# The gate branch's b tiles and the convolution's projection as pairs, in a new order with attention in larger portions

## The chip, the core and the metric

The kernel runs on one core of a Trainium2 chip. Its metric is the device time of one execution in microseconds. Engines are named as in the profile: PE (TensorE matmuls), PEld (its weight loads), DVE (VectorE), ACT (ScalarE), POOL (GpSimd), SP (SyncE, which only issues transfers here). L109 and the like are lines of the kernel before. L109 is the line of the helper through which nearly all of the ordered instructions go, so groups of that line are told apart by the names of their tiles.

## What is computed

One decoder layer on 512 prompt tokens and 8 x 8 sample tokens (576 columns in all), float32, with D_MODEL = 1024 and D_FF = 2816. Attention is a sliding window of 128 with 16 heads and 4 key/value heads.

```
mod = silu(c) @ w_ada + b_ada                      # sh1, sc1, g1, sh2, sc2, g2
h = rmsnorm(x, norm1_g) * (1 + sc1) + sh1
b, c, xa, q, k, v, ga, gb = split(h @ w_in)        # columns 0, 1024, 2048, 3072, 4096, 4352, 4608, 5632
u  = c * xa
ya = (b * causal_conv3(u)) @ w_conv_out            # convolution branch
o  = sliding_window_attention(q, k, v, sinks)      # with ALiBi
yb = o @ w_attn_out
x  = x + g1 * ((sigmoid(ga) * ya + sigmoid(gb) * yb) @ w_mix_out)
h2 = rmsnorm(x, norm2_g) * (1 + sc2) + sh2
a, val = split(h2 @ w_up)
x  = x + g2 * ((gelu(causal_conv3(a)) * val) @ w_down)
y  = rmsnorm(x, final_g)
```

The last inputs of the two convolutions and the last 128 key and value rows are outputs too.

## The kernel before

**Layout.** Activations lie transposed: a tile has 128 features on the partitions and the 576 tokens (NT) along a row, so `h` is a list of 8 tiles (NK), each as a high and a low part. `split` makes them: ACT copies the source, rounded, into the high part, and DVE subtracts that from the source for the low part. A product is taken in three passes (high x high, high x low, low x high).

**Unpaired products.** `product(w, xs)` makes one tile of 128 output features: 8 steps over k, each of 3 passes on 2 groups of tokens (256 and 320), so 48 matmuls into two PSUM banks. `weights` loads a 1024 x 128 block of weights (512 KB, `raw`, by SP) and splits it into `whi` and `wlo`.

**Pairs.** `pair_product` makes two output tiles at once by a Strassen-like scheme of 7 half products instead of 8. The halves are over the output tiles, over k (0 to 3 and 4 to 7) and over the tokens (HT = 288 each). Each of the 7 parts is 4 k-steps of 3 passes on 288 columns, 84 matmuls in all, which accumulate into the banks X, Z and Y; between parts ACT negates a bank into the next (`minus`), or hands a finished quarter to the caller (`out_a0`, `out_b1`, `out_a1`, `out_b0`). The scheme needs sums of weights: `pair_weights` makes from the two raw blocks the split tiles A (first part, `a0` and `a1`), B (`s1`, `b1`), C (`s2`, `s4`), all 128 x 1024, and D (`s3`, 128 x 512). The second part uses B, the third C. It needs sums of the activations too: `PairOperands`, for each k pair (k, k + 4), adds and subtracts halves on DVE and splits the results (`th`/`tl`, `nh`/`nl`, and `n3`, which overwrites half of h's own tile).

A pair's weight parts are made during the pair before: `steps` maps a part's number to what is issued there on ACT and DVE (`in_turn`: sums and A at 0, B at 2, D at 3, C at 4 or 5). From the gates to tile 3 of attention's projection PE, ACT and DVE run in the order in which the program is written (`pinned`); elsewhere a scheduler may move DVE's and ACT's unpinned instructions.

**Fillers.** `tick()` is called after every k-step. It adds a rate to a sum, and when the sum reaches 1 it takes the next portion of a generator: this is how attention's and the modulation's small matmuls get between the products' matmuls in PE's order. `drain()` issues what is left.

**The stages that the change touches**, in order of time:
1. for each m of 8: the c tile, the x tile (u = c * xa and its convolution: `conv`, two taps on DVE), and the b tile (`conv_times`, split into `g`), each an unpaired product. Beside them, at a rate of 0.58 per tick, `attention`: 16 prompt units (4 key heads x 4 blocks), each as `prompt_scores` (three portions, the last with the softmax) and `prompt_values` (three portions), where the values of a unit come behind the scores of the next; then two decode units. The four aux PSUM banks are shared by them.
2. the convolution's projection: 8 unpaired products of `w_conv_out` with g. Beside them `modulation(2048)` as a filler: rows of w_ada (`ada`, 256 KB each, by SP; two sets ahead), four small matmul groups of 16 at L1100. `PairOperands` of h are made from m = 3 on.
3. eight gate pairs (columns 4608 for the convolution branch, 5632 for attention's), whose sigmoids stay in SBUF; the convolution's tiles are multiplied by theirs (`gated`). In the last pair attention's output is split (`part_o`, tiles `oh` and `ol`).
4. attention's projection: 8 unpaired products of `w_attn_out`, gated and added to ya; beside them `modulation(4096)`, begun at a rate of 2 in 28 during the last pair, then at 11 in 60.
5. x, which the output projection's residual needs, is read back from DRAM into the two tiles that `ot` and `o` had (L1330, 2 x 1152 KB on POOL's queue). Then the output projection and the FFN, whose up-projection is of pairs too, with a convolution and a GELU beside them.

Of the kernel before, what the change touches and what calls it, by code (L numbers as in the profile page):

```python
# [16 lines left out]
P = 128  # L17
# [52 lines left out]
def step_kernel(ctx: ExitStack, tc: tile.TileContext, ins: dict, outs: list):  # L70
# [19 lines left out]
    def slot(s, dt=F32, shape=None):  # L90
        return ap_.tile(shape or [P, NT], dt, tag="a", name=nm(s))
# [31 lines left out]
    def pv(t):  # L123
        return t[:, 0:512]
# [49 lines left out]
    def fill(gen, rate):  # L174
        filler[:] = [gen, rate, 0.0]

    ticks = [0]

    def tick():

        ticks[0] += 1
        if filler:
            filler[2] += filler[1]
            while filler and filler[2] >= 1.0:
                filler[2] -= 1.0
                if next(filler[0], True):
                    filler.clear()
# [94 lines left out]

    def pair_weights(ra, rb):

# [49 lines left out]
    def pair_product(w, x, steps, out_a0, out_a1, out_b0, out_b1):  # L334
# [19 lines left out]

# [616 lines left out]

    def prompt_scores(hd, i, ss, _):
        while 4 * hd + 3 not in QS or ticks[0] < ready[hd]:
            yield False
        w = 256 if i else P
        k0 = (i - 1) * P if i else 0
        ss += [slot("s", shape=[P, 2, 256]) for _ in range(2)]
        kh, kl = (x[:, k0 : k0 + 256] for x in KS[hd])
        for x in range(2):
# [6 lines left out]
            for e in range(2):  # L986
# [4 lines left out]
                )  # L991
            yield False
        softmax(ss, 4, snk[:, 4 * hd : 4 * hd + 4], nsnk[:, 4 * hd : 4 * hd + 4], w)
        yield False

    def prompt_values(hd, i, ss, _):
        nkt = 2 if i else 1
        pts = []
        for kt in range(nkt):
# [10 lines left out]
        yield False  # L1010
        yield False
        O = aux()
        for n in range(2 * nkt):
# [7 lines left out]
            if n:  # L1021
                tc.keep_in_program_order(done)
        yield False
# [4 lines left out]
        yield False  # L1028

    def attention():  # L1030
        units = [(prompt_scores, prompt_values, (hd, i)) for hd in range(4) for i in range(4)]
        units += [(decode_scores, decode_values, (q,)) for q in range(2)]
        before = None
        for n, (sc, va, arg) in enumerate(units + [(None, None, None)]):
            s, more = [], []
            if n in CACHE_AT:
                cache_load(CACHE_AT.index(n))
            if sc is not None:
                yield from sc(*arg, s, more)
            if before is not None:  # L1040
                yield from before
            before = va(*arg, s, more) if va is not None else None


# [101 lines left out]

    def modulations():
        yield from modulation(4096)
# [9 lines left out]
    gcv = []  # L1158
    for m in range(NK):
# [22 lines left out]
        nc.scalar.copy(c_sb, ps)  # L1182
        ps = product(weights(kpm(w_in, 2048 + m * P), NK), h)
        u = padded()
        nc.vector.tensor_tensor(out=u[:, 2:514], in0=pv(ps), in1=pv(c_sb), op=ALU.mult)
        nc.vector.tensor_tensor(
            out=b10(u)[:, :, 2:10], in0=b8(sv(ps)), in1=b8(sv(c_sb)), op=ALU.mult
        )
        keep_state(u, m)
        y = conv(u, parT[:, 64 + m : 65 + m], parT[:, 72 + m : 73 + m], parT[:, 80 + m : 81 + m], stT[:, m, :])  # L1190
        ps = product(weights(kpm(w_in, m * P), NK), h)
        gcv.append(split_slot(conv_times(ps, y), "g"))
    state_out(NK, ncv_p[:], ncv_s[:])


    def sigmoid_pair(w, steps):

        sa, sb = slot("sg"), slot("sg")

        def sigmoid(out, src):  # L1200
            act.activation(out, src, AF.Sigmoid)

        def a0(ps):
            sigmoid(sa[:, :HT], ps)

        def b1(x, y, op):
            dve.tensor_tensor(out=sb[:, HT:], in0=x, in1=y, op=op)

        def a1(x, y, op):
            sigmoid(sb[:, HT:], sb[:, HT:])  # L1210
            dve.tensor_tensor(out=sa[:, HT:], in0=x, in1=y, op=op)

        def b0(ps):
            sigmoid(sb[:, :HT], ps)
            sigmoid(sa[:, HT:], sa[:, HT:])

        pair_product(w, made["op"], steps, a0, a1, b0, b1)
        return [sa, sb]

    ya, made = [], {}  # L1220
    wco, wao = ins["w_conv_out"][0], ins["w_attn_out"][0]
    gate_cols = [c + m * P for c in (4608, 5632) for m in range(0, NK, 2)]
    raws = {}

    def gate_raws(n):
        if n < len(gate_cols):
            raws[n] = [load_w(kpm(w_in, gate_cols[n] + c), NK) for c in (0, P)]

    def conv_out(m, w):
        ps = product(w, gcv)  # L1230
        t = slot("ya")
        act.copy(t, ps)
        ya.append(t)

    for m in range(NK - 1):
        w = weights(kpm(wco, m * P), NK)
        if m >= 3:
            PairOperands(h, m - 3, made).all()
        conv_out(m, w)
    w_last = weights(kpm(wco, (NK - 1) * P), NK)  # L1240
    gate_raws(0)
    pinned += [pe, act, dve]
    w, steps = pair_weights(*raws[0])
    steps = in_turn(steps)
    for n in sorted(steps):
        steps[n]()
    gate_raws(1)
    conv_out(NK - 1, w_last)
    drain()
    sg, o = [], []  # L1250
    w_next = {}

# [3 lines left out]

    def gated(m):

        if sg[m] is not None:
            dve.tensor_tensor(out=ya[m], in0=ya[m], in1=sg[m], op=ALU.mult)  # L1260
            sg[m] = None

    for n in range(len(gate_cols)):
        if n + 1 < len(gate_cols):
            gate_raws(n + 2)
            after, steps = pair_weights(*raws[n + 1])
            steps = in_turn(steps, 5)
            if n >= 4:
                steps[1] = lambda m=2 * n - 8: gated(m)
                steps[4] = lambda m=2 * n - 7: gated(m)  # L1270
        else:
            w_next[0] = weights(kpm(wao, 0), NK)
            raw = load_w(kpm(wao, P), NK)
            steps = {
                0: lambda: gated(6), 1: lambda: gated(7), 3: lambda: part_o(2), 4: lambda: part_o(3),
                5: lambda: w_next.update({1: split_w(raw)}), 6: lambda: part_o(5), 7: lambda: part_o(7),
            }
        if n + 1 == len(gate_cols):
            fill(modulations(), 2 / 28)
        sg += sigmoid_pair(w, steps)  # L1280
        w = after
    part_o(NK)
    gb = sg[NK:]
    filler[1] = 11 / 60
    mixed = []
    for m in range(NK):
        if m + 1 < NK and m + 1 not in w_next:
            w_next[m + 1] = weights(kpm(wao, (m + 1) * P), NK)
        ps = product(w_next.pop(m), o)
        if m == 3:  # L1290
            pinned.clear()
        t = gb[m]
# [35 lines left out]
    x1t = [wp.tile([P, 4, NT], F32, tag="oh", name=nm("x1"), bufs=2) for _ in range(2)]  # L1328
    for x in range(2):
        nc.gpsimd.dma_start(x1t[x], xT_dram[x])  # L1330
    x1 = [x1t[k // 4][:, k % 4, :] for k in range(NK)]
# [516 lines left out]
```

## Time and profile before

| | |
|---|---|
| time, median of 3 runs (lowest, highest) | 1002.71 us (1002.39, 1004.38) |
| the profiled execution's own time | 1002.83 us |
| its span, from first to last instruction | 1001.1 us |
| mean granted clock of TensorE | 0.997 |
| DMA traffic | 119.18 MB, 119 GB/s on the mean |

The stages lie in that execution as follows (from the stretches of the trace; busy us of each engine):

| stage | from, to | PE | DVE | ACT |
|---|---|---|---|---|
| c, x and b tiles with attention | 72 to 324 | 251.79 | 153.61 | 121.80 |
| the convolution's projection | 324 to 383.5 | 59.50 | 30.82 | 18.18 |
| gate pairs | 383.5 to 472.7 | 89.20 | 64.07 | 52.04 |
| start of attention's projection | 473 to 498 | 21.38 | 9.25 | 5.69 |
| rest of it and of the output projection's start | 498 to 540 | 42.00 | 21.75 | 13.00 |

How to read the views: a group's row has line, engine, operation, out<-in with shapes and a count, then busy time and the mean time of one in ns, then the idle time of the engine ahead of these instructions and what ended it. A row of the chain of waits has a start, a length and what the time was spent on, so that consecutive rows are consecutive in time. A row of the DMA issues has the count, the size of each and the median time from issue to landing.

### The profile page before, as it was taken

The page shows a single profiled execution, that of the slowest core. Times are in us where ns is not written, and L with a number is a line of the kernel's source. Part 1 is how long each engine was busy: PE and PEld are TensorE (multiplying, and loading weights), DVE is VectorE, ACT ScalarE, POOL GpSimd, SP SyncE. Part 2 cuts the span into 40 slices and gives each one's busy share as a digit, 9 for nine tenths or more (in the row PEclk, how much of TensorE's full clock was granted, in tenths as well). Part 3 has the DMA queues.
Part 4 walks back from the last instruction along what each step waited for, and adds up shares of the span by engine and source line. Part 5 has one row for each costly group of instructions (what it writes and reads, how often), then busy time and mean ns, then how long its engine had stood idle before and what let it go on. Part 6 is the DMA issues. An engine that isn't in the chain of part 4 may idle for free.

```text
span 1001.1 us, 18626 instructions
## 1 busy us (share of the span) xinstructions
PE 983.0 (98%) x7516; PEld 943.0 (94%) x7516; DVE 642.2 (64%) x1183; ACT 465.2 (46%) x889; POOL 87.7 (9%) x253
## 2 busy tenths in 40 slices
PE   7999999999999999999899999999999999999997
PEld 5799999999999889999689999999999999999997
DVE  5737666666563366786364568995558975579663
ACT  6354545444544225556132338654226663246563
POOL 2222111100010000000000011100000000000020
PEclk9999999999999999999999999999999999999999
DMA  9983322333423822335962402233233322322212
GB/s 294 329 246 98 107 85 77 92 108 112 139 64 95 289 89 84 90 101 160 334 211 71 127 2 64 85 96 95 73 97 102 88 88 82 106 84 85 78 39 95
DMA packets 173480, 119.18 MB, mean 119 GB/s; under 512 B 6887, under 2 KB 160846, under 8 KB 173106
## 3 DMA queue, kind: packets, MB, share of 16 engines
q1 hardware_dynamic: 169954, 107.00, 35.0%
q0 software_dynamic: 3296, 10.73, 3.5%
q8 instruction: 59, 0.97, 0.4%
q14 instruction: 27, 0.22, 0.1%
q10 hardware_dynamic: 144, 0.26, 0.1%
HBM read 109.17 MB, written 7.35 MB: 116 GB/s over the span
## 4 chain that ended last, share of the span: by engine, by line
PE 93%; DMA 3%; issue 1%; SPq 1%; DVE 0%; ACT 0%; POOL 0%; POOLq 0%; DVEq 0%; ACTq 0%
PE mm L109 64%; PE aux L109 27%; PE aux L1100 2%; PE aux L1015 1%; DMA ad<-in_w_ada 1%; DMA ada<-in_w_ada 1%; SPq L381 1%; DMA x<-in_x_prompt 1%; ACT s L866 0%; POOL r L109 0%; DVE cs L388 0%; ACT hh L109 0%; DVE hl L109 0%; DVE yo L109 0%; DVE x L109 0%
## 5 line engine op out<-in xcount | busy, mean ns | idle before, releaser
L109 ACT ACTIVATE whi<-raw 128x1024 fp32r<-128x1024 f32 (+3 forms) x166 | 168.7, 1025 | 197.7 <-PE mm L109 109.8
L109 DVE TENSOR_TENSOR wlo<-raw,whi 128x1024 fp32r<-128x1024 f32 (+3 forms) x166 | 195.2, 1182 | 69.7 <-ACT whi L109 67.6
L109 PE MATMUL mm<-hh,whi 128*128 128x256 f32 (+1 forms) x528 | 118.1, 305 | 0.5 <-ACT hh L109 0.5
L109 PE MATMUL mm<-hh,wlo 128*128 128x256 f32 (+1 forms) x528 | 112.6, 295 | 0.0
L109 PE MATMUL mm<-hl,whi 128*128 128x256 f32 (+1 forms) x528 | 111.6, 295 | 0.1
L109 PEld LDWEIGHTS mm<-hh,whi 128*128 128x128 f32 x528 | 85.6, 188 | 8.1 <-issue 6.6
L109 PEld LDWEIGHTS mm<-hh,wlo 128*128 128x128 f32 x528 | 88.2, 188 | 0.0
L109 PEld LDWEIGHTS mm<-hl,whi 128*128 128x128 f32 x528 | 87.6, 188 | 0.7 <-DVE hl L109 0.5
L109 PE MATMUL aux<-2l,whi 128*128 128x288 f32 (+2 forms) x232 | 68.6, 296 | 0.0
L109 PE MATMUL aux<-2h,wlo 128*128 128x288 f32 (+2 forms) x232 | 68.6, 295 | 0.0
L109 PE MATMUL aux<-2h,whi 128*128 128x288 f32 (+2 forms) x232 | 68.4, 295 | 0.0
L109 PE MATMUL mm<-fh,whi 128*128 128x256 f32 (+1 forms) x304 | 64.8, 295 | 0.3 <-DVE rt L109 0.3
L109 PE MATMUL mm<-fl,whi 128*128 128x256 f32 (+1 forms) x304 | 65.0, 295 | 0.0
L109 PE MATMUL mm<-fh,wlo 128*128 128x256 f32 (+1 forms) x304 | 65.0, 294 | 0.0
L109 DVE SCALAR_TENSOR_TENSOR x<-mm,modT,x 128x512 f32<-128x512 f32 (+1 forms) x33 | 22.6, 685 | 66.0 <-PE mm L109 65.8
L109 PEld LDWEIGHTS mm<-fh,whi 128*128 128x128 f32 x304 | 50.6, 188 | 0.6 <-PE aux L109 0.6
L109 PEld LDWEIGHTS mm<-fh,wlo 128*128 128x128 f32 x304 | 50.9, 188 | 0.0
L109 PEld LDWEIGHTS mm<-fl,whi 128*128 128x128 f32 x304 | 50.8, 188 | 0.0
L866 ACT ACTIVATE s<-s,nmx 128x256 f32<-128x256 f32 (+1 forms) x72 | 34.1, 475 | 25.5 <-DVE nmx L863 17.4
L109 PEld LDWEIGHTS aux<-2h,whi 128*128 128x128 f32 x232 | 43.7, 188 | 0.0
L109 PEld LDWEIGHTS aux<-2l,whi 128*128 128x128 f32 x232 | 43.7, 188 | 0.0
L109 PEld LDWEIGHTS aux<-2h,wlo 128*128 128x128 f32 x232 | 43.6, 188 | 0.0
(314 smaller groups left out, 2581.5 us busy)
## 6 DMA issues: line engine op xcount, KB each, us to landing
raw<-in_w_in SPq DMA_DIRECT2D x52, 512.0 KB, 4.1
raw<-in_w_up SPq DMA_DIRECT2D x44, 512.0 KB, 3.7
ada<-in_w_ada SPq DMA_DIRECT2D x64, 256.0 KB, 6.0
ad<-in_w_ada SPq DMA_DIRECT2D x32, 256.0 KB, 6.1
raw<-in_w_down SPq DMA_DIRECT2D x16, 512.0 KB, 3.4
raw<-in_w_conv_out SPq DMA_DIRECT2D x8, 512.0 KB, 3.5
raw<-in_w_attn_out SPq DMA_DIRECT2D x8, 512.0 KB, 3.6
raw<-in_w_mix_out SPq DMA_DIRECT2D x8, 512.0 KB, 5.7
```

The source lines that it names most:

```text
L109: done = getattr(self.engine, name)(*args, **kwargs)
L381: return tc.keep_in_program_order(nc.sync.dma_start(dst, src))
L866: nc.scalar.activation(s[x // 2][:, x % 2, :w], s[x // 2][:, x % 2, :w], AF.Exp, bias=nmx[:, x : x + 1], accum_out=den[:, x : x + 1],)
L1015: done = nc.tensor.matmul(O[HALF[par], :256], vt(i - nkt + 1 + kt)[:, hd * 64 : hd * 64 + 64], pts[kt][:, par * 256 : par * 256 + 256], st ...
L1100: done = nc.tensor.matmul(ps[32 * j : 32 * j + 32, :], cT[:, k, :], cols[k][j], start=(k == 1), stop=(k == NK - 2),)
```

## The change

- **Order.** The b tiles leave the c/x loop. After c and x come 16 pairs, called jobs: 4 of b tiles (0 to 3), 4 of the gates of attention's branch (4 to 7, columns 5632), 4 of the gates of the convolution's branch (8 to 11, columns 4608), 4 of the convolution's projection (12 to 15). Each job's weights are loaded two jobs ahead and prepared one job ahead.
- **Pairs.** The b tiles and the projection's tiles were unpaired and become pairs. h's `PairOperands` are now made at m = 5 and 6 of the c/x loop, all but `n3`, which job 0 makes (h's own tiles are still needed till then). The projection's operands come from g in plain float32 (`RawOperands`) in small steps laid out by `plan` over jobs 8 to 12.
- **Low parts by DMA.** In `pair_weights`, for the names in `moved`, the low part isn't subtracted on DVE: ACT writes the negated high part into it and POOL's queue adds the source with an accumulating transfer. This is for B and D of the weights of jobs 0 to 4 and 9 to 15.
- **Steps.** D moves to step 3 with the second sums behind it, B to step 1, C's high part to 4 and its low part to 5.
- **Gates.** Sigmoids are stored to DRAM (`sg_dram`, POOL's queue) and read back by SP (`gate`) when they are needed.
- **Fillers.** Attention runs beside c/x alone, a unit in two larger portions (at a rate of 0.3: the scores and softmax; then the values of the unit three before and the transposes of the one two before); decode then at 0.35 and the modulation at 12 in 70. A tick in a pair counts half. `modulation(4096)` starts only after the last job.
- **x's reload** is put under `issue_after` of the tile m = 4 of attention's projection (`x1_after`, a DVE instruction).

```diff
-    def tick():
+    def tick(share=1.0):
         ticks[0] += 1
         if filler:
-            filler[2] += filler[1]
+            filler[2] += filler[1] * share
...
+    class RawOperands:
...
+        def sums(self):
+            (r0, r1), a, b = (self.r0, self.r1), slice(0, HT), slice(HT, NT)
+            self.t = t = slot("tw")
+            dve.tensor_tensor(out=t[:, a], in0=r0[:, a], in1=r0[:, b], op=ALU.subtract)
+            dve.tensor_tensor(out=r0[:, b], in0=r0[:, b], in1=r1[:, b], op=ALU.subtract)
+            dve.tensor_tensor(out=t[:, b], in0=r1[:, b], in1=t[:, a], op=ALU.add)
+        def first(self):
...
+            act.activation(self.x0[0], self.r0, AF.Copy)
...
+        def first_low(self):
...
+            self.low(self.x0, self.r0)
+            dve.tensor_tensor(out=self.r0[:, a], in0=self.r1[:, a], in1=self.t[:, b], op=ALU.subtract)
+        def second(self):
...
+            act.activation(self.tt[0], self.t, AF.Copy)
...
+        def third(self):
...
+            act.activation(self.x1[0], self.r1, AF.Copy)
...
+            act.activation(self.n4[0], self.r0[:, a], AF.Copy)
...
+        def third_low(self):
+            self.low(self.x1, self.r1)
+            self.low(self.n4, self.r0[:, :HT])
...
         def low(name, src):
             hi, lo = w[name]
-            dve.tensor_tensor(out=lo, in0=src, in1=hi.bitcast(F32), op=ALU.subtract)
+            if name in moved:
+                act.activation(lo, hi.bitcast(F32), AF.Copy, scale=-1.0)
+                pool.dma_start(lo.bitcast(F32), src, accum_op=ALU.add)
+            else:
+                dve.tensor_tensor(out=lo, in0=src, in1=hi.bitcast(F32), op=ALU.subtract)
...
-                tick()
+                tick(0.5)
...
     def attention():
...
+        for n in range(len(units) + 3):
...
+            if n < len(units):
+                hd, i = units[n]
+                while 4 * hd + 3 not in QS or ticks[0] < ready[hd]:
+                    yield False
+                s[n] = prompt_scores(hd, i)
+            yield False
+            if n >= 3:
+                prompt_values(*units[n - 3], pts.pop(n - 3))
+            if 2 <= n <= len(units) + 1:
+                pts[n - 2] = prompt_turn(units[n - 2][1], s.pop(n - 2))
+            yield False
+        filler[1] = .35
...
     def beside_conv():
         yield from attention()
-        filler[1] = 13 / 76
+        filler[1] = 12 / 70
         yield from modulation(2048)
         yield True
-    fill(beside_conv(), 0.58)
+    fill(beside_conv(), .3)
+    sg_dram = dp.tile([2, NK, P, NT], F32, name="sg_dram")
...
+        def prepare(self, moved=""):
+            self.w, t = pair_weights(*self.raws, moved=moved)
+            order = {0: "sums1 ah al", 1: "bh bl", 3: "dh dl sums2", 4: "ch", 5: "cl"}
...
+    def branch_outs(m):
+        ts, ys = [slot("g") for _ in range(2)], ycv[m : m + 2]
...
+        def second_half(e, x, y, op):
+            t, v = ts[e], ys[e]
+            dve.tensor_tensor(out=t[:, HT:], in0=x, in1=y, op=op)
+            dve.tensor_tensor(out=t[:, HT:512], in0=t[:, HT:512], in1=v[:, HT:512], op=ALU.mult)
+            nc.gpsimd.tensor_tensor(out=b8(sv(t)), in0=b8(sv(t)), in1=b10(v)[:, :, 0:8], op=ALU.mult)
...
+    def gate_outs(x, m):
...
+        def b0(ps):
+            sigmoid(tb[:, :HT], ps)
+            sigmoid(ta[:, HT:], ta[:, HT:])
+            for e, t in enumerate((ta, tb)):
+                pool.dma_start(sg_dram[x, m + e], t)
...
+    jobs = [Job(w_in, m * P, made, lambda m=m: branch_outs(m)) for m in range(0, NK, 2)]
+    jobs += [
+        Job(w_in, c + m * P, made, lambda x=x, m=m: gate_outs(x, m))
+        for x, c in ((1, 5632), (0, 4608)) for m in range(0, NK, 2)
+    ]
+    jobs += [Job(wco, m * P, made_g, lambda m=m: conv_outs(m)) for m in range(0, NK, 2)]
...
-        ps = product(weights(kpm(w_in, 1024 + m * P), NK), h)
+        w = weights(kpm(w_in, 1024 + m * P), NK)
+        if m in (5, 6):
+            operands(2 * m - 10)
+        ps = product(w, h)
...
+        w = weights(kpm(w_in, 2048 + m * P), NK)
+        if m in (5, 6):
+            operands(2 * m - 9)
+        if m == NK - 1:
+            jobs[0].load()
+            pinned += [pe, act, dve]
+            for fs in jobs[0].prepare("BD").values():
+                for f in fs:
+                    f()
+            jobs[1].load()
+        ps = product(w, h)
...
-        ps = product(weights(kpm(w_in, m * P), NK), h)
-        gcv.append(split_slot(conv_times(ps, y), "g"))
...
+    jobs[0].before = {2: [op.n3 for op in hp], 3: [taps]}
+    jobs[3].before = {2: [lambda: state_out(NK, ncv_p[:], ncv_s[:])]}
+    plan = {
+        8: {2: "0sums", 3: "0first", 4: "0first_low", 6: "0second", 7: "0second_low"},
+        9: {2: "1sums", 3: "1first", 4: "1first_low", 6: "1second", 7: "1second_low"},
+        10: {2: "2sums", 6: "2first 2second", 7: "2first_low 2second_low"},
+        11: {
+            2: "3sums", 3: "3first", 4: "3first_low 3second", 5: "3second_low",
+            6: "0third 1third", 7: "0third_low 2third",
+        },
+        12: {0: "1third_low", 1: "2third_low", 2: "3third 3third_low"},
+    }
...
+    for n, job in enumerate(jobs):
+        if n + 2 < len(jobs):
+            jobs[n + 2].load()
...
+        steps = jobs[n + 1].prepare("BD" if n < 4 or n > 7 else "") if n + 1 < len(jobs) else {}
+        outs = job.outs()
+        pair_product(job.w, job.ops["op"], joined(job.before, steps, job.after), *outs)
+    drain()
+    fill(modulations(1), 11 / 60)
     mixed = []
+    gb = {m: gate(1, m) for m in range(2)}
     for m in range(NK):
...
         ps = product(w_next.pop(m), o)
...
+        if m + 2 < NK:
+            gb[m + 2] = gate(1, m + 2)
         dve.tensor_tensor(out=t, in0=ps, in1=t, op=ALU.mult)
-        dve.tensor_tensor(out=t, in0=t, in1=ya[m], op=ALU.add)
+        done = dve.tensor_tensor(out=t, in0=t, in1=ya[m], op=ALU.add)
+        if m == 4:
+            x1_after = done
         mixed.append(split_slot(t, "mx"))
...
-    for x in range(2):
-        nc.gpsimd.dma_start(x1t[x], xT_dram[x])
+    with tc.issue_after(x1_after.ins):
+        for x in range(2):
+            nc.gpsimd.dma_start(x1t[x], xT_dram[x])
```

More of the change, by code (lines that the diff above doesn't have):

```diff
@@ L1145, in modulation, with modulations @@
         yield False
[L1147 to L1148 removed]
+    def modulations(n):
+        yield from modulation((2048, 4096)[n])
         yield True
@@ new lines, in copy_outs, with total, gate, conv_outs @@
+    def copy_outs(ts):
+        ta, tb = ts
+        def total(t):
+            return lambda x, y, op: dve.tensor_tensor(out=t[:, HT:], in0=x, in1=y, op=op)
+        return (
+            lambda ps: act.copy(ta[:, :HT], ps), total(ta), lambda ps: act.copy(tb[:, :HT], ps), total(tb),
+        )
+    def gate(x, m):
+        t = slot("gt")
+        nc.sync.dma_start(t, sg_dram[x, m])
+        return t
+    ya, w_next, o, late = [], {}, [], []
+    def conv_outs(m):
+        gs = [gate(0, m + e) for e in range(2)]
+        ts = [slot("ya") for _ in range(2)]
+        ya.extend(ts)
+        late.extend(
+            lambda t=t, g=g: dve.tensor_tensor(out=t, in0=t, in1=g, op=ALU.mult) for t, g in zip(ts, gs)
+        )
+        return copy_outs(ts)
@@ L1159, in step_kernel, with operands @@
+    jobs = [Job(w_in, m * P, made, lambda m=m: branch_outs(m)) for m in range(0, NK, 2)]
[4 more added lines that the diff above has]
+    jobs += [Job(wco, m * P, made_g, lambda m=m: conv_outs(m)) for m in range(0, NK, 2)]
+    hp = [PairOperands(h, kp, made) for kp in range(4)]
+    def operands(kp):
+        hp[kp].sums()
+        hp[kp].high()
+        hp[kp].low()
     for m in range(NK):
@@ L1220, in step_kernel @@
[L1220 to L1251, printed above, removed]
+        def taps(u=u, m=m):
+            ycv.append(
+                conv(u, parT[:, 64 + m : 65 + m], parT[:, 72 + m : 73 + m], parT[:, 80 + m : 81 + m], stT[:, m, :])
+            )
+        if m < NK - 1:
+            taps()
@@ new lines, in step_kernel @@
+    for n, at in plan.items():
+        jobs[n].after = {p: g_list(names) for p, names in at.items()}
+    n_conv = len(jobs) - 4
+    for n in range(4):
+        if n:
+            jobs[n_conv + n].before = {
+                1: [lambda n=n: late[2 * n - 2]()], 2: [lambda n=n: late[2 * n - 1]()],
+            }
+    jobs[-1].after = {
+        2: [lambda: part_o(2)], 3: [lambda: part_o(3)],
+        4: [lambda: w_next.update({1: split_w(w_raw)})], 5: [lambda: part_o(4)], 6: [lambda: part_o(6)],
+        7: [lambda: part_o(8)],
+    }
@@ L1255, in part_o @@
             o.append(split_slot(ot[k // 4][:, k % 4, :], "o"))
[L1257 to L1271, printed above, removed]
-            w_next[0] = weights(kpm(wao, 0), NK)
[L1273 to L1284, printed above, removed]
+    for n, job in enumerate(jobs):
+        if n + 2 < len(jobs):
+            jobs[n + 2].load()
+        elif n + 2 > len(jobs):
+            w_next[0] = weights(kpm(wao, 0), NK)
+            w_raw = load_w(kpm(wao, P), NK)
+        steps = jobs[n + 1].prepare("BD" if n < 4 or n > 7 else "") if n + 1 < len(jobs) else {}
[3 more added lines that the diff above has]
+    fill(modulations(1), 11 / 60)
     mixed = []
+    gb = {m: gate(1, m) for m in range(2)}
     for m in range(NK):
```

136 lines of the change are left out of this document (91 added, 45 removed).

## The prediction

> **What bounds the kernel now.** I read first the page's busy shares and its chain of waits, then the chain in order of time around the parts that change, then the stretches by stage and the groups by form.
>
> ```profile
> span 1001.1 us, 18626 instructions
> PE 983.0 (98%) x7516; PEld 943.0 (94%) x7516; DVE 642.2 (64%) x1183; ACT 465.2 (46%) x889; POOL 87.7 (9%) x253
> ...
> PE 93%; DMA 3%; issue 1%; SPq 1%; DVE 0%; ACT 0%; POOL 0%; POOLq 0%; DVEq 0%; ACTq 0%
> ```
>
> The chain that ends last is TensorE for 93%, so a matmul that isn't issued is time saved wherever the helpers keep up. Do they now? The stretches give the c/x/b products with attention (72 to 324), the gates (383.5 to 472.7), and for comparison an up-projection stretch whose pairs run beside a whole convolution and a GELU (590 to 687); then, around the start of attention's output projection, 473 to 498:
>
> ```profile
> 72.00:324.00 252.00, 251.79 (x1963) 236.79 (x1962) 153.61 (x372) 121.80 (x304) 29.37 (x64) 1.00 0.34 99
> ...
> 383.50:472.70 89.20, 89.20 (x674) 89.20 (x673) 64.07 (x87) 52.04 (x91) 0.00 (x0) 1.00 0.36 107
> ...
> 590.00:687.00 97.00, 97.00 (x732) 96.80 (x732) 83.56 (x161) 63.96 (x121) 13.39 (x46) 1.00 0.26 77
> ...
> 473.00:488.00 15.00, 11.38 (x83) 8.88 (x81) 5.75 (x8) 4.05 (x7) 0.88 (x2) 0.94 1.02 373
> 488.00:498.00 10.00, 10.00 (x73) 9.64 (x74) 3.50 (x4) 1.64 (x2) 0.00 (x0) 0.92 0.84 303
> ```
>
> The columns are length, then busy time of PE, PEld, DVE, ACT and POOL, the granted clock, DMA's share and GB/s. PE has no gap in the first three, with DVE at 61%, 72% and 86%. The one gap in the changed region is 473 to 488, where DMA is full (1.02, 373 GB/s). The chain shows why, and also gives the price of a matmul:
>
> ```profile
> 324.09 9.56 PE mm L109 x72
> ...
> 450.61 3.19 PE aux L109 x24
> ...
> 461.76 3.18 PE aux L109 x24
> ...
> 473.52 11.72 DMA ada<-in_w_ada
> 485.25 0.04 issue
> 485.29 2.75 PE aux L1100 x16
> 488.04 9.69 PE mm L109 x66
> 497.72 1.85 PE aux L1100 x16
> ```
>
> **Part by part.** *Fewer matmuls.* An unpaired product of one tile is 8 k-steps of 3 passes on 2 token groups, 48 matmuls; a pair is 7 parts of 4 k-steps and 3 passes, 84 instead of 96. One matmul takes 9.56/72 = 0.1328 us unpaired and 3.18/24 = 0.1325 in a pair (both have 288 columns on the mean; the pair's own period is 461.76 - 450.61 = 11.15 = 84 x 0.1327). Eight b tiles and eight projection tiles make eight pairs: 8 x 12 = 96 matmuls x 0.1328 = **-12.7 us**. The built order of PE shows exactly 96 matmuls fewer.
>
> *The modulation's loads.* PE stood still for w_ada rows, and ran slower behind it:
>
> ```profile
> PE aux L1100 <- DMA ada<-in_w_ada: 3.6, 1, 3.6
> ...
> POOL x L1330 <- DVE ol L109: 148.4, 2, 145.0
> ...
> x<-xT_dram POOLq DMA_DIRECT2D x2, 1152.0 KB, 8.5
> ada<-in_w_ada SPq DMA_DIRECT2D x64, 256.0 KB, 6.0
> ```
>
> The wait is 3.6 us; the first 16 ada matmuls then took 2.75 instead of 1.85 (0.9), and the 66 matmuls behind them 9.69 instead of 66 x 0.1328 = 8.76 (0.9): 5.4 in all, in the stretches with a granted clock of 0.94 and 0.92. [...] The ada rows were starved by the reload of x (2 x 1152 KB), which POOL issues when the last low parts of o (ol) are done. Here the change does not do what it says: `issue_after` orders only instructions on the engine of the one it is given, x1_after is on DVE and the load on POOL's queue; in the built order the two loads still wait for ol and for nothing later, and with o split inside the last pair they start about 2 us sooner or later than now. But the ada loads themselves move: the filler starts after the last pair at 11/60 per tick, so rows 0 and 1 are issued at ticks 6 and 11 (4.8 and 8.8 us into the projection) and used at tick 22 (17.5 us). The reload, 8.5 us a half, is over by about 11 us. That leaves rows(1), the later one, 8.7 us (17.5 - 8.8) for a load whose median is 6.0: I take the whole **-5.4**, bounds 0 and -5.4. On SP they now share the queue with the gates' reloads, 288 KB a tile; more than 5.4 can't be gained, for the wait goes once.
>
> *VectorE and ScalarE beside c/x.* Rows for what leaves and comes:
>
> ```profile
> L109 DVE TENSOR_TENSOR wlo<-raw,whi 128x1024 fp32r<-128x1024 f32 x154 | 187.4, 1220 | 68.3 <-ACT whi L109 66.2 <-PE aux L109 1.6 <-issue 0.2
> L109 DVE TENSOR_TENSOR raw<-raw 128x512 f32<-128x512 f32 x52 | 36.9, 709 | 1.7
> L109 DVE TENSOR_TENSOR wl<-s,wh 128x512 fp32r<-128x512 f32 x26 | 17.7, 682 | 0.0
> L109 DVE TENSOR_TENSOR cy<-mm,y 128x512 f32<-128x512 f32 x12 | 8.2, 687 | 15.4 <-PE mm L109 15.3
> L109 DVE TENSOR_TENSOR tl<-tw,th 128x576 fp32r<-128x576 f32 x8 | 6.0, 756 | 5.7 <-ACT th L109 5.7
> L109 DVE TENSOR_TENSOR t<-t,tw 128x288 f32<-128x288 f32 x4 | 1.8, 451 | 0.0
> L109 ACT ACTIVATE whi<-raw 128x1024 fp32r<-128x1024 f32 x154 | 161.9, 1057 | 197.5 <-PE mm L109 109.8 <-DMA raw<-in_w_down 29.7 <-DVE raw L109 26.6
> L109 ACT ACTIVATE wh<-s 128x512 fp32r<-128x512 f32 x26 | 16.2, 622 | 0.0
> L109 ACT ACTIVATE th<-tw 128x576 fp32r<-128x576 f32 x8 | 5.5, 684 | 4.1 <-DVE tw L109 4.1
> L109 ACT COPY p<-aux 128x288 f32<-128x288 f32 x26 | 10.1, 390 | 13.1 <-PE aux L109 13.1
> L109 ACT ACTIVATE sg<-sg 128x288 f32<-128x288 f32 x16 | 7.1, 441 | 2.7 <-DVE sg L109 2.7
> ```
>
> b takes 8 x (1.22 + 0.69 + 0.2 + 0.76) = 23 us of DVE along with 8 x 6.37 = 51 of PE. The operands of h arrive from the projection's stretch, 4 x (3 x 0.76 + 5 x 0.45) = 18, and job 0's weights (A, C and the sums), 5. So 153.6 - 23 + 18 + 5 = 154 stand against 252 - 51 = 201: 77%, under the 86% at which the up-projection lost nothing. Attention's instructions are the same; its larger portions leave two portions' time between scores, softmax and transposes, so chains don't bind. But PE is in program order, the scores' four PSUM banks wait on DVE, and the operands come in one burst (tiles 5 and 6). Bounds 0 and, if two such bursts stall PE by one product's evacuation, 6; I take **+1.5**, near the up-projection row.
>
> *The low parts by DMA.* In 12 of the 16 pairs B's and D's low parts leave DVE (1.22 + 0.68) and become on ACT a negated copy (1.06 + 0.62) and on POOL an accumulating transfer of 512 and 256 KB from SBUF to SBUF, which no row shows. Its deadline: in a gate pair ACT spends the first 1.1 us on the previous pair's sigmoids, then the A copy 1.06, the negated X 0.4, B 1.06, its negative 1.06; with 0.5 of issue on POOL it starts 5.2 us into the pair. It is needed in the next pair's second part, by the third matmul: 11.15 + 1.6 (one part of 12) + 0.3 = 13.0, so there are **7.8 us of cover**. The nearest rows:
>
> ```profile
> L787 POOL DMA_DIRECT2D q<-low x16 | 8.4, 523 | 47.9 <-DVE low L783 20.5 <-PE aux L109 12.4 <-DVE den L873 7.3
> ...
> raw<-in_w_in SPq DMA_DIRECT2D x52, 512.0 KB, 4.1
> ...
> q<-low POOLq DMA_DIRECT2D x16, 128.0 KB, 3.2
> ...
> out<-in_cache_v_win POOLq DMA_DIRECT2D x1, 960.0 KB, 8.7
> ```
>
> 128 KB take 3.2 and 512 KB 4.1; with the destination read as well, at the same 2.3 us per MB, 5.3. The bounds are 3.2 and 8.7. I take 5.3, nearest to the row of the same size: hidden. [...] Pair 1 has less cover: in the built ACT order its B stands behind four high parts of h, a convolution tap and D, so its transfer starts some 10 us into job 0 and has about 6 us left: **+0.7** (0 to 3).
>
> *The convolution's operands.* Per k pair DVE gets 4.5 us and ACT 3 x 0.68 + 0.44 = 2.5, spread over jobs 8 to 12. A pair costs DVE 64.07/8 = 8.0 now, 6.1 without B and D, so at most 10.6 of 11.15 in job 11. ACT has 52.04/8 = 6.5 + 1.7 = 8.2 a pair, but job 11 holds first, second and three thirds: 8.2 + 2 x 0.68 + 3 x 1.12 = 12.9, 1.8 over. What queues behind it is job 12's negated X, without which its third part can't accumulate, and the last x10 operand. Instructions on ACT overlap their neighbours a little, and job 12 has slack before 3.2 us: **+1.0** (0 to 3). Sigmoids stored on POOL and read back on SP (16 x 288 KB) add some 50 GB/s to a stage at 107; a reload is needed two tiles after its issue, so nothing.
>
> *Sum.* The profiled execution took 1002.83 (span 1001.1 and 1.7 around it), 0.1 above the median of the three runs. 1002.8 - 12.7 - 5.4 + 1.5 + 0.7 + 1.0 = 987.9: **988**, 984 with no stall at all.
>
> **Rivals.** *The transfers come late* (slower): every moved pair waits in its second part for B's low part. For it: an unseen kind of transfer, beside 1 MB of weights a pair; ada rows took up to 12 us when another queue's transfer ran. Against: at 36% DMA share the rows stay near 4. The rest of the sum gains 15; over 11 pairs that is gone at 1.35 us each, so it decides from 7.8 + 1.35 = 9.2 us of transfer; at 10 us, 11 x 2.2 = 24, **1012**. *Queues bind*: DVE beside c/x and ACT in the operand pairs cost the upper bounds, 6 + 3 + 3 instead of 3.2: **997**, up to 1001 with transfers a little late. For it: job 11 is over its period already. *The reload still collides*: the ada rows keep waiting, since x isn't reloaded later: 988 + 5.4 = **993**.
>
> **Chances.** Forecast 0.52, reload 0.13, queues 0.19, late transfers 0.16. About 0.02 each of the last two end within 0.2% (2 us, what a measurement of this kernel can tell from no change): faster 0.52 + 0.13 + 0.17 = 0.82, same 0.04, slower 0.14. The range runs from no stall, 984, through the collision to the queues' upper end, 1001; left out are the late transfers and a sliver below.
>
> **What would show it.** PE should have 96 matmuls fewer, be unbroken beside c/x, and have pairs every 11.15 us in jobs 2 to 10 and 13 to 15; jobs 1 and 12 show a short wait, on the DMA of wlo and on ACT. The wlo transfers should land in 5 to 6 us. No wait on ada rows over 1 us, and a granted clock of 1.00 after the last pair. It is wrong if PE waits for wlo in every moved pair, or on DVE before the first pair by more than 6 us.

## The result, and the profile after

The changed kernel takes 985.7 us (median of 5 runs, 985.28 to 986.5) against 1002.95 for the kernel before (5 runs): a ratio of 0.9825, 95% interval 0.9814 to 0.9836. The profiled execution took 986.5 with a span of 984.7. First the page's lines, then PE's waits in the changed kernel: in total, times, longest.

```profile
span 984.7 us, 18746 instructions
PE 968.7 (98%) x7420; PEld 929.1 (94%) x7420; DVE 670.2 (68%) x1247; ACT 505.2 (51%) x961; POOL 121.9 (12%) x301
...
PE 92%; DMA 4%; issue 2%; DVE 1%; ACT 0%; POOL 0%; SPq 0%; POOLq 0%; DVEq 0%
```

```profile
PE aux L109 <- DMA wlo<-raw: 1.2, 1, 1.2
PE aux L1173 <- DMA ada<-in_w_ada: 0.9, 1, 0.9
...
PE aux L109 <- DVE xl L109: 0.4, 1, 0.4
```

PE has 96 matmuls fewer (7516 to 7420), and between the end of c/x and the last pair only three waits, 2.5 us together: in jobs 3 (wlo), 4 (ada) and 12 (xl). The stretches of the changed kernel (c/x with attention; the 16 jobs; the first two stretches of attention's projection) have the same columns as in the prediction:

```profile
68.00:262.60 194.60, 194.60 (x1548) 182.07 (x1547) 144.90 (x370) 107.20 (x270) 32.72 (x70) 1.00 0.35 100
262.60:461.10 198.50, 195.99 (x1465) 186.38 (x1464) 132.37 (x206) 127.17 (x231) 34.93 (x52) 1.00 0.77 211
...
461.00:476.00 15.00, 15.00 (x114) 14.98 (x114) 8.98 (x13) 3.26 (x6) 1.10 (x2) 1.00 0.94 349
476.00:486.00 10.00, 10.00 (x78) 8.40 (x78) 4.64 (x6) 2.02 (x3) 0.00 (x0) 1.00 1.07 392
```

PE is unbroken beside c/x, and where it stood still before attention's projection it now runs at a clock of 1.00, although the DMA engines are as full there as they were (0.94 and 1.07).

To place the gain, take three marks from the rows of the tiles `hh` and `oh`: the first product on h, the first and the last product of attention's projection. In such a row stand the shortest, median and longest ns, then the first and the last start. Before:

```profile
L109 PE MATMUL mm<-hh,whi x528: 275/307/415, 22.0 to 322.4; 128*128 128x256 f32 x88, 128*128 128x320 f32 x88
L109 PE MATMUL mm<-oh,whi x128: 275/307/582, 472.8 to 538.0; 128*128 128x256 f32 x64, 128*128 128x320 f32 x64
```

and after:

```profile
L109 PE MATMUL mm<-hh,whi x400: 275/306/412, 22.5 to 261.8; 128*128 128x256 f32 x67, 128*128 128x320 f32 x67
L109 PE MATMUL mm<-oh,whi x128: 274/306/387, 462.7 to 522.2; 128*128 128x256 f32 x64, 128*128 128x320 f32 x64
```

| us | up to the first product on h | from there to the last pair | attention's projection | rest |
|---|---|---|---|---|
| before | 22.0 | 450.8 | 65.2 | 463.1 |
| after | 22.5 | 440.2 | 59.5 | 462.5 |

So -10.6 comes from the products up to the last pair, and -5.7 from attention's projection. The first and last columns, which the change doesn't touch, differ by half a microsecond either way; over all runs below they lie at 21.4 to 23.6 and 461.9 to 463.7. That is why the table is the finer reading and the times decide only from about 2 us.

The first product on h is itself a rough mark: the time from there to the last low part of h (`hl`), which no edit below touches, varies from 24.4 to 26.5 us over these runs. In the changed kernel that low part starts at 47.6:

```profile
L109 DVE TENSOR_TENSOR hl<-xn,hh x8: 757/758/760, 23.2 to 47.6; 128x576 fp32r<-128x576 f32 x8
```

From it to the first pair (262.4) takes 214.8 us in every kernel that has the change's portions of attention, and the 16 jobs then take 200.3 (to 462.7). Below, "the jobs" are counted from the first matmul of the first pair to the first product of attention's projection.

### The profile page after: what moved, and what is told of

Read it like the earlier page. It is cut to its first block, busy times and chain, and to the rows that moved or that the text cites. A ratio compares the mean times of both kernels' runs of the same rounds, so it can differ in the third digit from the quotient of the medians.

```text
span 984.7 us, 18746 instructions
## 1 busy us (share of the span) xinstructions
PE 968.7 (98%) x7420; PEld 929.1 (94%) x7420; DVE 670.2 (68%) x1247; ACT 505.2 (51%) x961; POOL 121.9 (12%) x301
## 4 chain that ended last, share of the span: by engine, by line
PE 92%; DMA 4%; issue 2%; DVE 1%; ACT 0%; POOL 0%; SPq 0%; POOLq 0%; DVEq 0%
PE mm L109 58%; PE aux L109 31%; PE aux L1173 2%; PE aux L1078 1%; DMA ad<-in_w_ada 1%; DMA wlo<-raw 1%; DMA ada<-in_w_ada 1%; DMA raw<-in_w_in 1%; DMA x<-in_x_prompt 0%; DVE xl L109 0%; DVE wlo L109 0%; POOL r L109 0%; ACT whi L109 0%; SPq L446 0%; DVE cs L453 0%
## 5 line engine op out<-in xcount | busy, mean ns | idle before, releaser
L109 PE MATMUL mm<-hh,whi 128*128 128x256 f32 (+1 forms) x400 | 88.4, 302 | 0.5 <-ACT hh L109 0.5
L109 PE MATMUL mm<-hh,wlo 128*128 128x256 f32 (+1 forms) x400 | 85.2, 294 | 0.0
L109 PE MATMUL mm<-hl,whi 128*128 128x256 f32 (+1 forms) x400 | 84.4, 295 | 0.1
L109 PEld LDWEIGHTS mm<-hh,whi 128*128 128x128 f32 x400 | 65.5, 188 | 2.4 <-ACT hh L109 1.0
L109 PEld LDWEIGHTS mm<-hl,whi 128*128 128x128 f32 x400 | 66.2, 188 | 0.7 <-DVE hl L109 0.5
L109 PEld LDWEIGHTS mm<-hh,wlo 128*128 128x128 f32 x400 | 66.8, 188 | 0.0
L109 PE MATMUL mm<-fh,wlo 128*128 128x256 f32 (+1 forms) x304 | 65.2, 295 | 0.0
L109 DVE TENSOR_TENSOR raw<-raw 128x512 f32<-128x512 f32 x68 | 47.4, 698 | 2.4
L109 PE MATMUL aux<-hh,whi 128*128 128x288 f32 (+2 forms) x160 | 46.8, 301 | 0.0
L109 PE MATMUL aux<-hl,whi 128*128 128x288 f32 (+2 forms) x160 | 45.9, 295 | 0.0
L109 PE MATMUL aux<-hh,wlo 128*128 128x288 f32 (+2 forms) x160 | 45.9, 295 | 0.0
```

The costliest lines, as they stand in the source:

```text
L109: done = getattr(self.engine, name)(*args, **kwargs)
```

## The experiments

**The two main terms.** The first four kernels were timed beside the kernel before, which took 1003.44 there.

*Modulation later, in the kernel before.*

```diff
-        if n + 1 == len(gate_cols):
-            fill(modulations(), 2 / 28)
...
-    filler[1] = 11 / 60
+    fill(modulations(), 11 / 60)
```

> The kernel before, with one thing of the change: modulation(4096) starts only after the last gate pair, at 11 in 60 per tick. Theory (x's reload starved its rows, and a later start is enough): the wait of 3.6 us and the slow matmuls behind it go, 1003.0 - 5.4 = 997.5. Rival (the reload still collides, as it starts where it did): the wait only moves to the next groups, 1002 to 1003.

997.21 against 1003.44, ratio 0.9941 (0.9928 to 0.9954). Attention's projection takes 59.4 instead of 65.2. The two stretches that had the gap, now in this kernel:

```profile
473.00:488.00 15.00, 15.00 (x115) 15.00 (x114) 7.31 (x11) 4.82 (x9) 0.80 (x2) 1.00 1.01 365
488.00:498.00 10.00, 10.00 (x79) 8.40 (x78) 4.91 (x6) 3.24 (x4) 0.00 (x0) 1.00 0.73 258
```

DMA is as full as before (1.01), but nobody waits for it. The later start of this filler alone, without any pair, is worth a third of the whole.

*Modulation early again, in the changed kernel.*

```diff
         outs = job.outs()
+        if n + 1 == len(jobs):
+            drain()
+            fill(modulations(1), 4 / 28)
...
-    drain()
-    fill(modulations(1), 11 / 60)
+    filler[1] = 11 / 60
```

> The changed kernel with the first two portions of modulation(4096) put back into the last pair, as in the kernel before. Theory: the wait on ada rows comes back, 985.7 + 3.6 to 5.4 = 989 to 991. Rival (the wait went because something else about the last pair changed, such as when the reload starts): 985 to 986.5.

993.45, ratio 0.9898 (0.9882 to 0.9914): 7.7 us above the changed kernel, and 2.5 above the upper end of what was expected. The wait is back, and behind it the slow matmuls, as the chain and the stretch show:

```profile
463.83 12.16 DMA ada<-in_w_ada
475.99 0.04 issue
476.04 3.64 PE aux L1173 x16
479.68 9.81 PE mm L109 x66
```

```profile
476.00:486.00 10.00, 9.96 (x57) 6.99 (x58) 1.19 (x2) 0.00 (x0) 0.00 (x0) 0.72 1.06 392
```

The longest wait is 4.4 us, and the clock then 0.72: 16 matmuls take 3.64 instead of 1.85, and the 66 behind them 9.81 instead of 8.76. In the kernel before it was 3.6 us, and 2.75 and 9.69. So the cost of the longer wait was put too low.

*The same, with x's reload really later.* DVE writes a column of each of the reload's tiles first, from tile m = 4 of the projection:

```diff
-    with tc.issue_after(x1_after.ins):
...
+        m4 = mixed[4][0].bitcast(F32)[:, 0:1]
+        nc.vector.tensor_tensor(out=x1t[x][:, 0, 0:1], in0=m4, in1=m4, op=ALU.add)
         nc.gpsimd.dma_start(x1t[x], xT_dram[x])
```

> As the run with modulation(4096) begun in the last pair, and x's reload now made to wait in earnest: DVE first writes one column of each of its tiles from tile m = 4 of attention's projection. Theory (the reload is the cause): no wait on ada rows, 985 to 987. Rival (the cause is that SP's queue or the buffers of the rows are full at that place): as without the later reload, 989 to 991.

986.83 (0.9818 to 0.9846), projection 59.8, no wait on these rows. So the collision with the reload is the cause, and there are two cures: rows later or reload later. The change has the first: its first matmul on these rows starts at 480.3, against 471.4 here. Its `issue_after` cures nothing: its reload is issued 461.9 and 465.7 us into the execution, at the start of the projection, and not behind tile 4.

*A part more in each new pair.* `pair_product` gets a flag `twice`:

```diff
+            if twice and at == 0:
+                part(bank, wn, xn_, False, False)
             part(bank, wn, xn_, at > 1)
...
+        pair_product(..., twice=n < 4 or n > 11)
```

> The changed kernel with the first part of each of the eight new pairs (b tiles and convolution's projection) computed twice, 12 matmuls more in each, 96 in all; the bank is begun anew, so the values are the same. Theory (PE is the bound in all of them and a matmul costs 0.1328 us): + 12.7, less the 1.2 and 0.4 us of waits in jobs 4 and 12 that may now be covered: 997 to 998.5. Rival (these pairs are set by DVE, ACT or a transfer, and PE has slack in them): under + 6.

996.41, ratio 0.9929 (0.9917 to 0.9942): + 10.7 by the medians, 0.6 below the range that was expected. The jobs take 211.0 us instead of 200.3, again + 10.7. The waits for wlo and xl are gone (1.6), and the one for ada rows is 1.5 instead of 0.9, so the price of a matmul gives 12.7 - 1.6 + 0.6 = 11.7. So the new pairs are PE-bound but for about 1 us, and a matmul is worth some nine tenths of what it was priced at; the rival (under + 6) is out.

**The low parts, and attention's portions.**

*All low parts on DVE.*

```diff
-        steps = jobs[n + 1].prepare("BD" if n < 4 or n > 7 else "") ...
+        steps = jobs[n + 1].prepare("") ...
...
-            for fs in jobs[0].prepare("BD").values():
+            for fs in jobs[0].prepare().values():
```

> The changed kernel with all low parts of weights on DVE again (no negated copies on ACT, no accumulating transfers). My theory (the pairs are set by PE and DVE has room): DVE gets 1.9 us more in each of 12 pairs, about 10.6 of 11.15 in jobs 8 to 10 and 11.8 in job 11; job 4's wait of 1.2 for the transfer goes, job 12's of 0.4 grows to some 1.5: 985 to 987. Rival (the moves are what keeps DVE from binding): up to 1.9 us in each of the pairs, 990 to 1005.

991.83, ratio 0.9883 (0.9867 to 0.9898): 6.1 slower than the change, more than I expected. But it isn't 1.9 a pair either. PE's waits and three stretches (job 0, twice, and job 11) show where:

```profile
PE mm L109 <- DVE hl L109: 3.0, 1, 3.0
PE aux L109 <- DVE xl L109: 1.4, 2, 1.0
PE mm L109 <- ACT mm L109: 1.0, 1, 1.0
```

```profile
262.00:274.00 12.00, 8.78 (x66) 8.32 (x64) 7.84 (x17) 8.63 (x22) 0.85 (x2) 1.00 0.20 59
274.00:286.00 12.00, 10.89 (x73) 9.71 (x74) 11.24 (x20) 3.81 (x12) 0.98 (x2) 1.00 0.34 93
408.00:420.00 12.00, 11.82 (x89) 11.59 (x88) 11.83 (x19) 8.42 (x16) 1.07 (x2) 1.00 0.48 151
```

In job 0 h's last operands (`n3`, here `hl`) stand behind the weights' low parts on DVE; in jobs 11 and 12 DVE is at its limit. Jobs without such extra work lost at most 0.2 us each. The jobs take 204.8 instead of 200.3, and PE's waits explain 3.4 of these 4.5 us; the rest shows in no wait, and stays open.

*B's low part later.* Two parts later (step 3, as shown), and three (step 4, ahead of C):

```diff
-            order = {0: "sums1 ah al", 1: "bh bl", 3: "dh dl sums2", 4: "ch", 5: "cl"}
+            order = {0: "sums1 ah al", 1: "bh", 3: "bl dh dl sums2", 4: "ch", 5: "cl"}
```

> The changed kernel with B's low part made at step 3 instead of 1, two parts (3.2 us) later. By the trace the transfer is issued 5.6 us into a pair, takes 4.4 and is needed 13.0 us after the pair's start: 3.0 us to spare. Theory (that is all its cover): 0.2 to 0.6 us in 11 pairs, 986 to 992. Rival (a late transfer is covered elsewhere): 985.7.

> The changed kernel with B's low part made at step 4 instead of 1, three parts (4.8 us) later, behind D on ACT. Theory: issued some 10.6 us into a pair and landed at 15, 2 us too late in each of 11 pairs: about + 21, 1003 to 1011. Rival (covered elsewhere, or only the first late pair costs): under 990.

At step 3: 988.58, ratio 0.985 (0.9835 to 0.9865), PE waits once for wlo, 1.8 us. At step 4: 1000.65, ratio 0.9972 (0.9961 to 0.9984), where PE's wait is

```profile
PE aux L109 <- DMA wlo<-raw: 9.4, 9, 3.8
```

So a transfer put two parts later is still covered (the jobs take 201.3, 1.0 longer), one put three parts later isn't, and then nearly all of the gain is gone. The mean wait, 9.4 / 9 = 1.0 us, is half of the 2 that I expected. The jobs are 12.0 longer (212.3). PE's waits there grow by 8.4, from 2.5 to 10.9, and behind the one of 3.8 us PE ran slow, at 0.57 from 310 to 314 (18 matmuls in 4.00 us, against 2.47 in the changed kernel); the rest of the loss shows in no wait of the trace.

*Attention in its old portions.* The generators of the kernel before, at a rate at which attention ends at the same place in PE's order:

```diff
-    fill(beside_conv(), .3)
+    fill(beside_conv(), 0.75)
```

> The changed kernel with attention in the portions of the kernel before (three of the scores, three to four of the values, the values right behind the next unit's scores), at a rate of 0.75 per tick, which ends them at the same place. My theory (beside c/x PE is the bound, and chains of attention are covered with either): 985 to 988. Rival (with only 128 ticks instead of 192 the smaller portions follow so closely that their chains of scores, softmax, transposes and values stall PE): 16 units of 0.5 to 1 us, 994 to 1002.

1001.29, ratio 0.9975 (0.9963 to 0.9987): my expectation missed by 13 us, and the rival's number came out. In the waits, and in the stretches around the operands of h (made at m = 5 and 6):

```profile
PE aux L1080 <- ACT pt L1073: 9.8, 4, 6.4
```

```profile
160.00:180.00 20.00, 19.24 (x148) 17.80 (x147) 14.27 (x36) 11.47 (x31) 2.97 (x5) 1.00 0.28 81
...
200.00:220.00 20.00, 19.42 (x149) 18.11 (x148) 14.49 (x38) 9.89 (x28) 1.52 (x2) 1.00 0.32 98
220.00:240.00 20.00, 13.61 (x86) 12.24 (x85) 12.12 (x31) 7.37 (x18) 0.80 (x3) 0.83 0.37 129
```

The mechanism isn't quite the rival's: up to 200 us the small portions cost 0.76 in all. It is where the operands stand in DVE's queue that PE waits 6.4 us for ACT's copy of the transposed probabilities (`pt`), and then runs at 0.83. From h's last low part to the first pair it takes 230.0 instead of 214.8, and the jobs 1.3 more; this execution is the slowest of twelve (998.57 to 1004.17). Two more kernels asked whether the bursts are needed.

```diff
-        if m in (5, 6):
-            operands(2 * m - 10)
+        if 3 <= m <= 6:
+            operands(m - 3)
```

> The run with attention's old portions, with the operands of h made one k pair per tile at m = 3 to 6 instead of two at m = 5 and two at m = 6. Theory (the stalls there come where the bursts of operands on DVE, nl, tw and tl, queue ahead of the softmax that the next matmuls wait for): most of the 9.8 us of waits on ACT's pt and of the slow clock behind them go, 987 to 992. Rival (the smaller portions follow too closely by themselves, wherever the operands are): 996 to 1003.

998.93, ratio 0.9957 (0.9944 to 0.997): spreading the operands helps little (224.2 up to the first pair). PE still waits:

```profile
PE aux L1080 <- ACT pt L1073: 7.5, 5, 3.2
```

Then all four k pairs of operands behind the c/x loop:

```diff
     gp = []
+    for kp in range(4):
+        operands(kp)
```

> The run with attention's old portions, with all operands of h made only behind the c/x loop, so that none stands beside attention; the first pairs must then wait for them, which by itself costs up to four times 4.5 us of DVE and a slow restart, so the reading is the waits of PE on ACT's pt beside c/x and not the time. Theory (a burst of operands is needed for the stalls, since without one the same portions cost 0.76 us from 72 to 180 us): under 1.5 us of waits on pt, and PE unbroken from 180 to 255. Rival (the small portions at 0.75 per tick stall PE by themselves): the waits on pt stay at 7 to 10 us.

1009.3, as PE now waits 11.9 us for the operands themselves; but beside c/x

```profile
PE aux L1080 <- ACT pt L1073: 1.9, 3, 0.8
```

That is near the theory (under 1.5), and far from 7 to 10, though PE isn't unbroken behind 180 us, as the theory had it (it waits 0.6 twice). So the small portions hardly stall PE without the operands, and the operands don't stall it with the larger portions; together they do, in two bursts or in four. The larger portions bought the room that the operands of h use: without it 15.6 of the gain's 17.2 us are lost. The change's portions are larger and also further apart (a unit's values come three units behind its scores); which of the two does it was not tried.

**Towards a faster version.** The waits for wlo and for ada rows fall together with the loads of modulation(2048), so it was slowed down, and in a second kernel one step of g's operands was moved from job 11 to job 10 too.

```diff
-        filler[1] = 12 / 70
+        filler[1] = 6 / 70
```

> The changed kernel with modulation(2048) at 6 in 70 instead of 12 in 70. Theory (job 4's wait of 1.2 for B's low part and the wait of 0.9 for ada rows are both the rows' loads, 8 x 256 KB at once, sharing the DMA engines with the transfer): both go, 983.6. Rival (the transfer is late for another reason): 985 to 986, and above that if the rows, spread over ten jobs, now disturb others.

> The changed kernel with modulation(2048) at 6 in 70 and the third step of the first k pair of g moved from the end of job 11 to job 10, the others one place up. Theory: job 12's wait of 0.4 on DVE's xl, which stood behind ACT's crowded job 11, goes too: 983.2. Rival (ACT in job 11 only passes it on to something else): as with the slower modulation alone.

985.67 (ratio 0.9816 to 0.9844) and 985.54 (0.9813 to 0.9839), no different from the change. Both waits on transfers are gone from the trace in both, and the wait for xl falls from 0.4 to 0.2 in the second. The jobs take 199.0 and 198.8 instead of 200.3, so 1.3 and 1.5 us less where 2.1 and 2.5 were expected; the profiled runs' other parts vary by as much. There is no proof here of a faster kernel.

## Why the prediction was right

- **Fewer matmuls, -12.7: right.** The count is exact. From h's last low part (47.4 in the kernel before) to attention's projection it is 425.4 before and 415.1 after, -10.3, and -12.7 with the 2.5 us of waits is -10.2. Put back, 96 matmuls cost 10.7, where price and waits give 11.7.
- **The modulation's loads, -5.4: right.** It measured -5.7 in the change and -5.8 alone (65.2 to 59.4). That the later reload is none was right too, and the rival in which the reload still collides failed. The rows' first use lies where it was put (17.6 us into the projection, forecast 17.5), but their loads don't: SP issues rows 0 and 1 from 462.2 and 465.5 on, 0.5 us before and 2.8 us after the projection's start, and not 4.8 and 8.8 us into it. So they lie beside the reload, and it is the later use that saves them. Gaps of 3.6, 4.4 and 6.4 us were each followed by a lower clock (0.92, 0.72, 0.83 in the stretches), and the changed kernel, whose gaps there are at most 1.2, has 1.00. But in these traces the length of a gap alone doesn't settle whether the clock falls, as the last section shows.
- **DVE and ACT beside c/x, +1.5: too much; its lower bound, 0, came out.** PE waits nowhere, with DVE at 74% (144.90 of 194.60) where 77% was set, and the sum of the first point leaves nothing for this term. Up to the first pair the changed kernel needs 214.8 us from the last low part of h (47.6 to 262.4), and the one with old portions and no operands 218.1, or 216.2 without its waits: the larger portions save about 1.4 even there. I passed over the portions in one clause, "so chains don't bind"; that was true, and it was the condition for nearly all of the gain.
- **Transfers hidden: right, with one exception.** These are the issues of the changed kernel with their median us to landing, and the spread for B's low parts (`wlo`):

```profile
wlo<-raw POOLq DMA_DIRECT2D x12, 512.0 KB, 4.4
sg_dram<-sg POOLq DMA_DIRECT2D x16, 288.0 KB, 4.1
gt<-sg_dram SPq DMA_DIRECT2D x16, 288.0 KB, 5.2
...
wl<-s POOLq DMA_DIRECT2D x12, 256.0 KB, 3.7
```

```profile
DMA to landing us min/median/max: 4.4/4.4/9.6
```

  The estimate was 5.3, and it is 4.4 at the median. This is B's issue in job 9, which begins at 383.74, and the one in job 2:

```profile
388.30 0.89 POOL L109 DMA_DIRECT2D wlo<-raw  x1 [2.52 <-ACT p L109]
...
298.46 0.87 POOL L109 DMA_DIRECT2D wlo<-raw  x1 [7.79 <-ACT p L109]
```

  So B's transfer is issued 4.6 us into a pair in jobs 8 to 11, 13 and 14 (4.5 to 4.7; the estimate was 5.2), and 5.8 in job 12. It is needed at 13.0, so 4.0 (13.0 - 4.6 - 4.4) are to spare there. The expectation of the run at step 3, with 5.6 us and 3.0 to spare, doesn't come out of this trace. With the transfer at step 3 the issue comes 6.7 us into a pair, and 6.7 + 4.4 = 11.1 is still in time. The exception is not job 1, for which 0.7 was set (its transfer lands in time), but job 3, which some expectations call job 4. In the chain it is the first of these two waits; the second, for ada rows, is in job 4:

```profile
298.46 9.61 DMA wlo<-raw
...
308.12 2.47 PE aux L109 x18
...
316.65 8.03 DMA ada<-in_w_ada
...
324.72 1.92 PE aux L1173 x16
```

  and SP's queue at that time:

```profile
294.12 0.54 SPq L1189 DMA_DIRECT2D ada<-in_w_ada  x1
...
296.09 3.43 SPq L1189 DMA_DIRECT2D ada<-in_w_ada  x7
...
309.32 8.27 SPq L1189 DMA_DIRECT2D ada<-in_w_ada  x8
```

  Eight row loads are issued as the transfer starts; it takes 9.61, over the point of 9.2 from which the prediction's slower rival decides, and costs 1.2. With the slower modulation four loads stand there, and the same transfer takes 4.9. This rival happened once in eleven pairs. The prediction argued against it from rows of 4 us at a DMA share of 36%; over the jobs the share is 0.77, so the transfers stayed near 4.4 on fuller DMA engines than it reckoned with. I had looked at this filler only at its other place, after the last pair; its own wait of 0.9 in the jobs is missing from the sum.
- **Job 12, +1.0: 0.9**, of which 0.4 is a wait. The job takes 12.0 us, the other projection jobs 11.1. The wait is at one of the two places named: xl, behind ACT's crowded job 11 (10.87 of 11.5 us busy from 408 to 419.5). But ACT is busy for 10.5 us of job 11, where 12.9 was set.

The sum was 987.9 for the profiled execution, which took 986.5. Of these 1.4 us, 0.7 are stalls (PE's waits are 2.5 where 3.2 were set), 0.3 is the modulation, and the rest is no more than what the untouched start and end differ by. That the stalls' sum came so near is partly luck: +1.5 beside c/x and 0.7 in job 1 came out as 0, and 1.2 in job 3 and 0.9 in job 4 were not foreseen there. The pairs take 11.1 to 11.2 us from job 7 on (but for job 12), while jobs 0 to 5 take 12.8 to 15.6, as decode's and the modulation's small matmuls stand in them. The order of the jobs, and b's pairs apart from the projection's, were not tried by themselves.

## What to carry to other kernels

A saving of matmuls on a full TensorE is worth nearly its count (96 put back cost 10.7 us where the price gave 12.7), but only as long as the helpers' chains keep their distance: here the same 96 matmuls fewer made their stages 6.3 us longer with attention's small portions (457.1 against 450.8 between the marks, in the slowest execution of that kernel), and all low parts on DVE cost a third of the whole gain. When operands are put beside a filler, ask how long the filler's own chain may be delayed, and rather give it larger portions further apart before spreading the operands. A stall on a load was cured here by needing its data later (the projection took 59.4 instead of 65.2) and by moving the transfer that it met (59.8 instead of 67.0); check in the trace what a move really moves.

## What the runs showed that was not expected

A single wait can cost more than its length: the 4.4 us of waiting in the projection became 7.5 (67.0 against 59.5) through the clock of 0.72 behind it.

In these traces the length of a wait alone doesn't settle whether it costs clock. Waits of 2.0 us (operands behind the loop), 2.1 and 2.4 us (old portions) were followed by a lower clock: 0.51 from 333.5 to 337, 0.57 from 247 to 251 and 0.58 from 326 to 330. Waits of 3.0 (all low parts on DVE) and 3.2 us (operands spread) were not: 1.00 from 275 to 279 and from 243 to 247. Behind the 2.1 us the next 12 matmuls of a product took 2.63 us, behind the 3.2 us 1.79. What decides it was not tried here.

A transfer of 512 KB from SBUF into SBUF that adds to its destination took 4.4 us at the median, 0.7 more than the 3.7 for 256 KB: by an estimate from these two alone, most of it doesn't depend on the size.
